# Sums of w_down's quarters: from accumulating DMAs spread over the attention stages to GpSimd additions beside the first span's w_up products

## The chip, the cores and the metric

The kernel runs on one core of a Trainium2 chip. The metric is the device time of one execution in microseconds (us). The kernel before was timed in three runs: 2850.33, 2852.82 and 2859.31 us, so its median is 2852.82 us. The engines are named as the profile names them: PE (matrix products), PEld (PE's weight load), DVE (VectorE), ACT (ScalarE), POOL (GpSimd) and SP (the queue that starts nearly all DMAs).

## The reference, cut to what matters

One layer over 2048 prompt rows and 32 sample rows: projections, dilated attention and a gated MLP branch, then the feed-forward part, which is what the change concerns:

```python
h2 = rms_norm(x, norm_pre_ffn)
f = jnp.square(jax.nn.relu(h2 @ w_up)) @ w_down      # w_up 1024x4096, w_down 4096x1024, float32
x = x + rms_norm(f, norm_post_ffn)
```

## The kernel before

**Spans and stages.** The rows are worked in two spans: span 0 is 1024 prompt rows and the 32 sample rows, span 1 the other 1024. First come attention and gated branches of span 0, then those of span 1; then `ffn()` runs `up(0)` (w_up products of span 0), `down(0)`, `up(1)` and `down_rows(1)`. Every float32 product is made of three products of float32r parts (high and low).

**Seven products for eight.** In `ffn()` each matrix is cut in four quarters, and a product of two such matrices is made of seven products of quarters or of sums of quarters (`SEVEN`, line 50). On the weight side four sums are needed, named in `SUMS`: s1 = a21 + a22, s2 = a11 + s1, s3 = a11 + a21, s4 = a12 + s2. The sums depend on the weights alone. They are made ahead and laid in DRAM: `gate_sums` (of a part of w_in), `up_sums` and `down_sums` (four forms of 2048x512 each).

**How the sums are made before.** `weight_sums()` (line 1425) lists 4 blocks of w_in, 8 of w_up and 8 of w_down. For each block and each of its four sums it issues two DMAs: a plain copy DRAM to DRAM on SP's queue (line 1454), and an addition done by the DMA itself, issued by POOL with `accum_op=add` (line 1459). The generator stands in lane 3; `pace` (line 310) takes one step of it each time 3600 columns have gone through PE. So these DMAs are spread over the attention and gate stages; those of w_down come last, beside span 1's attention, its gated branch and its seven-product gates (`mix_seven`). `ffn()` empties lane 3 before its first product.

**Lanes.** A lane is a queue of generators. `tick()` takes a step of lanes 0, 1 and 2; `up` calls it twice in each of its 112 products (16 column groups by 7 forms). What a step of lane 2 issues is kept behind what stands already on PE, DVE, ACT and POOL (`ORDERED`); SP is not among them, and there the program's scheduler sets the order.

**The stream of weights in `up(0)`.** `weight_stream` (line 1512) loads two forms (128x512 each) into one of two `raw` tiles by two DMAs on SP's queue (line 283). For each form ACT casts the high part into a `wf` tile (line 1509) and POOL subtracts to get the low part (line 1510). There are four `wf` tiles. A product then takes 24 matrix instructions (line 1599) into one of three PSUM tiles `pd`, which DVE or ACT add into `ov` (lines 1606 and 1608). After the sixth and the seventh form of a column group the results go to DRAM in `f` (lines 1636 and 1639). At the same time lane 1 carries `moved()` and `differences(1)`, which make span 1's input `h2` and its differences `hd` (lines 385, 1377, 1467 to 1472).

**Small tiles that the change uses.** The pool `sm` has two tiles of 128x1024 floats with the tags `t` and `gbc` and one buffer each. They hold scratch rows and gain rows in other stages; during `up(0)` the kernel before uses neither, but for the load of the last gain into `gbc` (line 451).

Of the kernel before, what the change touches and what calls it, by code (L numbers as in the profile page):

```python
# [10 lines left out]
F32 = mybir.dt.float32  # L11
F32R = mybir.dt.float32r
AF = mybir.ActivationFunctionType
ALU = mybir.AluOpType
# [4 lines left out]
P = 128  # L19
D = 1024  # L20
# [38 lines left out]
    ("s4", "b22", ((X12, X12),)),  # L59
)  # L60
SUMS = ("s1", "s2", "s3", "s4")
DIFFS = ("t1", "v", "t3", "t4")


# [48 lines left out]
def hybrid_step(ctx: ExitStack, tc: tile.TileContext, ins: dict, outs: list):  # L113
    nc = tc.nc
# [92 lines left out]
    def push(lane, gen):  # L207
        lanes[lane].append(gen)
        return gen
# [28 lines left out]
    def drain(lane, gen=None):  # L238

        while (lanes[lane] if gen is None else gen in lanes[lane]) and step(lane):  # L240
            pass
# [1186 lines left out]
    def weight_sums():  # L1428
# [5 lines left out]
        def by_rows(name, dst):  # L1434
            w = ins[name][0]
            hk, hm = w.shape[0] // 2, w.shape[1] // 2
            n = hk // 8
            for q in range(8):
                u, l = slice(q * n, (q + 1) * n), slice(hk + q * n, hk + (q + 1) * n)
                todo.append(parts(w[u, :hm], w[l, :hm], w[u, hm:], w[l, hm:], [dst[i, u] for i in range(4)]))  # L1440
# [5 lines left out]
            u, l = slice(q * P, (q + 1) * P), slice(512 + q * P, 512 + (q + 1) * P)  # L1446
            todo.append(parts(w[u, ca], w[l, ca], w[u, cb], w[l, cb], [gate_d[i, u] for i in range(4)]))
        by_rows("w_up", up_d)
        by_rows("w_down", down_d)
        for n in range(len(todo) + 2):  # L1450
            for i in range(4):
                if n < len(todo):
                    with tc.issue_after(load[0].ins):
                        nc.sync.dma_start(todo[n][i][0], todo[n][i][1])
                    yield

                j = n - (2 if i == 3 else 1)
                if 0 <= j < len(todo):
                    nc.gpsimd.dma_start(todo[j][i][0], todo[j][i][2], accum_op=ALU.add, max_dma_last_dim=8192)
                    yield  # L1460

    def differences(s):

# [35 lines left out]
    def down_form(form, k, nk, m, nm):  # L1499

        if form in SUMS:
            src = down_d[SUMS.index(form), k * P : (k + nk) * P, m : m + nm]
        else:
            i, j = int(form[1]) - 1, int(form[2]) - 1
            src = ins["w_down"][0][j * 2048 + k * P : j * 2048 + (k + nk) * P, i * 512 + m : i * 512 + m + nm]
        return src.rearrange("(k p) m -> p k m", p=P)
# [17 lines left out]
    def ffn():  # L1524
# [293 lines left out]
        ops.update(prepare(0, ("s2",), forms[6:]))  # L1818
        for gen in later:
            push(1, gen)  # L1820
        up(0, ops)
        drain(0)
        drain(1)
        ops1 = {}
        gain_last = {}

# [123 lines left out]
```

## Time and profile before

| | |
|---|---|
| median of 3 runs | 2852.82 us |
| the profiled execution | 2853.56 us |
| its span from first to last instruction | 2851.9 us, so 1.7 us lie around it |
| PE busy | 2805.7 us, 98% of the span |
| POOL busy | 1329.6 us, 47% |
| DVE / ACT busy | 1375.0 us / 1288.6 us |
| DMA | 550.95 MB, mean 193 GB/s |
| `up(0)` | from about 1546 to 1873 us of the span |

A row of the windows view gives a stretch of the span, its length, the busy time of PE, PEld, DVE, ACT and POOL (with the number of instructions), the granted PE clock as a share, the mean busy share of the core's 16 DMA engines and the GB/s that they moved. A row of the waits view names who waited, for whom, and us in total, times, and the longest. A row of the groups view gives line, engine, operation, tiles and shapes, the count, then busy us and mean ns of one. The chain of waits is followed back from the last instruction.

### The profile page before, as it was taken

Reading aid. Unit: us, or ns where it says so; the run is one execution under the profiler, and the core shown is the slowest. Engines: PE = TensorE matmul, PEld = TensorE weight load, DVE = VectorE, ACT = ScalarE, POOL = GpSimd, SP = SyncE. Lnnn points to the kernel's source line nnn. Section 1 sums busy time; section 2 is a strip of 40 time slices with the busy share of each in tenths; the row PEclk is TensorE's granted clock in tenths of the full one; section 3 lists DMA queues with packets and bytes.
Section 4 is the critical chain, followed back from the end, with each engine's and each line's share of the span. In section 5 each row is a group of like instructions: output and inputs, shape, how many; then the busy total and the mean of one; then the engine's idle time right before and its main releaser. Section 6 shows DMA issues by size and latency. Waiting matters only on the chain.

```text
span 2851.9 us, 45811 instructions
## 1 busy us (share of the span) xinstructions
PE 2805.7 (98%) x17350; PEld 2551.3 (89%) x17350; DVE 1375.0 (48%) x2318; ACT 1288.6 (45%) x2519; POOL 1329.6 (47%) x1167
## 2 busy tenths in 40 slices
PE   8999999999999999999999999999999999999998
PEld 8999999999988888877888999999999888888887
DVE  4557464752544434554555546442424644452225
ACT  5444452213654444433346544453434544554334
POOL 3346434564123444444761444455546644445553
PEclk9999999999999999999999999999999999999999
DMA  4344345875677665499867878676656766586665
GB/s 140 104 126 136 93 126 162 221 203 152 206 196 217 167 157 150 121 221 271 227 177 253 278 233 297 197 257 194 214 177 218 235 202 193 185 283 195 190 188 169
DMA packets 486606, 550.95 MB, mean 193 GB/s; under 512 B 28273, under 2 KB 373425, under 8 KB 476658
## 3 DMA queue, kind: packets, MB, share of 16 engines
q1 hardware_dynamic: 472992, 502.60, 55.0%
q0 software_dynamic: 13248, 45.36, 8.7%
q8 instruction: 137, 2.24, 0.3%
q14 instruction: 83, 0.68, 0.1%
q10 hardware_dynamic: 146, 0.07, 0.0%
HBM read 425.54 MB, written 206.27 MB: 222 GB/s over the span
## 4 chain that ended last, share of the span: by engine, by line
PE 84%; DVE 6%; DMA 5%; ACT 2%; issue 2%; POOL 1%; SPq 0%; DVEq 0%; POOLq 0%; ACTq 0%
PE pg L323 25%; PE pd L1599 22%; PE pe L1599 11%; PE pe L1707 10%; PE pg L337 5%; PE pg L1236 2%; PE pu L757 2%; PE pt L743 1%; DMA gbc<-in_cache_kv_w_dram 1%; PE ps L323 1%; PE ps L709 1%; DMA raw<-in_w_in_dram 1%; PE ps L710 1%; POOL wf L1510 1%; PE pt L366 1%
## 5 line engine op out<-in xcount | busy, mean ns | idle before, releaser
L1510 POOL TENSOR_TENSOR wf<-raw,wf 128x512 fp32r<-128x512 f32 x493 | 699.8, 1426 | 725.8 <-ACT wf L1509 688.3
L323 PE MATMUL pg<-act,wh 128*128 128x352 f32 (+2 forms) x2976 | 796.4, 346 | 2.4 <-DVE xt L1292 1.4
L323 PEld LDWEIGHTS pg<-act,wh 128*128 128x128 f32 x2976 | 522.3, 189 | 32.5 <-DVE xt L1292 1.7
L1509 ACT CAST wf<-raw 128x512 fp32r<-128x512 f32 x493 | 304.7, 619 | 531.0 <-PE pd L1599 182.8
L323 PE MATMUL pg<-act,wl 128*128 128x352 f32 (+3 forms) x1488 | 512.5, 345 | 0.0
L303 POOL TENSOR_TENSOR wl<-raw,wh 128x512 fp32r<-128x512 f32 (+1 forms) x184 | 242.2, 1345 | 300.9 <-ACT wh L299 262.5
L1599 PE MATMUL pd<-act,wf 128*128 128x264 f32 x2880 | 361.2, 285 | 1.3 <-ACT ov L196 1.0
L1599 PEld LDWEIGHTS pd<-act,wf 128*128 128x128 f32 x2880 | 354.0, 189 | 2.0 <-ACT ov L196 1.4
L323 PEld LDWEIGHTS pg<-act,wl 128*128 128x128 f32 x1488 | 280.2, 188 | 17.1
L1707 PE MATMUL pe<-wf,act 128*128 128x512 f32 (+1 forms) x984 | 224.3, 389 | 1.4 <-ACT wf L1509 1.2
L1707 PEld LDWEIGHTS pe<-wf,act 128*128 128x128 f32 x984 | 181.7, 188 | 43.1 <-ACT wf L1509 1.4
L1608 DVE TENSOR_TENSOR ov<-pd,ov 128x528 f32<-128x528 f32 x140 | 96.2, 704 | 193.4 <-PE pd L1599 188.2
L1599 PE MATMUL pd<-pair,wf 128*128 128x264 f32 x1440 | 183.2, 284 | 0.0
L1599 PE MATMUL pe<-act,wf 128*128 128x512 f32 x768 | 182.6, 392 | 0.1
L1510 DVE TENSOR_TENSOR act<-flat,act 128x1024 fp32r<-128x1024 f32 (+1 forms) x76 | 102.1, 1346 | 162.4 <-ACT act L1509 162.4
L1599 PEld LDWEIGHTS pd<-pair,wf 128*128 128x128 f32 x1440 | 177.9, 188 | 0.0
L1599 PEld LDWEIGHTS pe<-act,wf 128*128 128x128 f32 x768 | 143.8, 188 | 32.9 <-ACT pair L1509 0.3
L299 ACT CAST wh<-raw 128x1024 fp32r<-128x1024 f32 (+1 forms) x91 | 91.7, 1009 | 173.3 <-PE pg L323 94.3
L1608 DVE TENSOR_TENSOR ov<-pe,ov 128x512 f32<-128x512 f32 x136 | 91.5, 687 | 137.3 <-PE pe L1599 126.4
L1599 PE MATMUL pd<-oa,wf 128*128 128x264 f32 x1056 | 135.0, 284 | 0.0
L715 ACT ACTIVATE ov<-ov 128x256 f32<-128x256 f32 (+1 forms) x192 | 91.8, 478 | 92.9 <-DVE ov L711 90.4
L1599 PEld LDWEIGHTS pd<-oa,wf 128*128 128x128 f32 x1056 | 130.8, 188 | 0.0
(340 smaller groups left out, 4619.4 us busy)
## 6 DMA issues: line engine op xcount, KB each, us to landing
raw<-in_w_in_dram SPq DMA_DIRECT2D x70, 512.0 KB
raw<-up_sums SPq DMA_DIRECT2D x128, 256.0 KB
raw<-down_sums SPq DMA_DIRECT2D x128, 256.0 KB
flat<-f SPq DMA_DIRECT2D x48, 528.0 KB
raw<-in_w_up_dram SPq DMA_DIRECT2D x96, 256.0 KB
raw<-in_w_down_dram SPq DMA_DIRECT2D x96, 256.0 KB
flat<-f SPq DMA_DIRECT2D x48, 512.0 KB
f<-ov SPq DMA_DIRECT2D x16, 1056.0 KB
```

The lines of the kernel that those rows point to most:

```text
L299: nc.scalar.copy(wh[:, :o], raw[:, :o])
L303: eng.tensor_tensor(wl[:, c], raw[:, c], wh[:, c].bitcast(F32), ALU.subtract)
L323: nc.tensor.matmul(pt[:, :n], a[:, o : o + P], b, start=(i == 0 and j == 0), stop=(i == last and j == 2))
L337: nc.tensor.matmul(pt[:n, o : o + width], a, b, start=(i == 0 and j == 0), stop=(i == last and j == 2))
L715: nc.scalar.activation(pb[:, h, :w], pb[:, h, :w], AF.Exp, scale=-1.0, bias=stats[:, u, h : h + 1], accum_out=stats[:, u, 2 + h : 3 + h],)
L757: nc.tensor.matmul(up[:, hs], tb[:, h, e * P : (e + 1) * P], vv[:, hs], start=(e == 0), stop=(e == len(rows) - 1),)
L1236: nc.tensor.matmul(pt, w[:, c, k], x[k][:, d], start=k == 0 and j == 0, stop=k == 3 and j == 2)
L1509: nc.scalar.copy(high, raw)
L1510: eng.tensor_tensor(low, raw, high.bitcast(F32), ALU.subtract)
L1599: nc.tensor.matmul(pt[:, o : o + n], w[:, a], x[:, b, c : c + n], start=first and j == 0, stop=last and j == 2)
L1608: nc.vector.tensor_tensor(X[to], res, X[add], ALU.add)
L1707: nc.tensor.matmul(pts[i][:, cs], x[k][:, c, t * P : (t + 1) * P], w[:, d, 0, cs], start=k == 0 and j == 0, stop=k == 15 and j == 2,)
```

## The change

`by_rows("w_down", ...)` is taken out of `weight_sums`, so lane 3 has 12 blocks left for 20. A new generator `down_sums` is pushed on lane 2 ahead of `up(0)`, and lane 2 is emptied behind it. It works in 32 blocks, each of 128 rows by 256 columns of every quarter. A block is loaded by two DMAs (2 x 256 KB) into the tile `t` or `gbc` in turn, POOL makes the four sums in place with four additions of 128x256, and one DMA of 512 KB stores all four to `down_sums`. The load of block n+2 into the same tile comes four steps behind the first additions of block n; a block takes six steps. The four forms lie in another order in DRAM (`DOWN_SUMS`). The rest of the sums (w_in, w_up) stay as they are.

```diff
+DOWN_SUMS = ("s2", "s4", "s3", "s1")
...
         by_rows("w_up", up_d)
-        by_rows("w_down", down_d)
...
+    def down_sums():
+
+        def fetch(n):
+            x = sm.tile([P, D], F32, tag=("t", "gbc")[n % 2], bufs=1, name="sums")
+            x = x.rearrange("p (i j m) -> p i j m", i=2, j=2)
+            k, c = n // 2, slice(n % 2 * 256, n % 2 * 256 + 256)
+            for j in range(2):
+                src = ins["w_down"][0][j * 2048 + k * P : j * 2048 + (k + 1) * P]
+                nc.sync.dma_start(x[:, :, j, :], src.rearrange("p (i m) -> p i m", i=2)[:, :, c])
+            return x, down_d[:, k * P : (k + 1) * P, c].rearrange("s p m -> p s m")
+
+        loaded = [fetch(0), fetch(1)]
+        for _ in range(6):
+            yield
+        for n in range(32):
+            x, dst = loaded[n]
+            a11, a12, a21, a22 = x[:, 0, 0], x[:, 0, 1], x[:, 1, 0], x[:, 1, 1]
+            nc.gpsimd.tensor_tensor(a22, a21, a22, ALU.add)
+            nc.gpsimd.tensor_tensor(a21, a11, a21, ALU.add)
+            yield
+            nc.gpsimd.tensor_tensor(a11, a11, a22, ALU.add)
+            nc.gpsimd.tensor_tensor(a12, a12, a11, ALU.add)
+            nc.sync.dma_start(dst, x.rearrange("p i j m -> p (i j) m"))
+            for _ in range(3):
+                yield
+            if n < 30:
+                loaded.append(fetch(n + 2))
+            yield
+            yield
...
-            src = down_d[SUMS.index(form), k * P : (k + nk) * P, m : m + nm]
+            src = down_d[DOWN_SUMS.index(form), k * P : (k + nk) * P, m : m + nm]
...
+        push(2, down_sums())
         up(0, ops)
-        drain(0)
-        drain(1)
+        for lane in range(3):
+            drain(lane)
```

In the changed kernel the new lines are 1470 (loads), 1479, 1480, 1482 and 1483 (additions) and 1484 (store); lines behind them are 30 higher than before (L1510 becomes L1540, L1599 L1629, L1636 and L1639 L1666 and L1669), lines between the two edits 1 higher (L283 becomes L284).

**POOL, as `up(0)` begins and in its last third.** Before, POOL ends the loads of w_out's parts (`wl`, `oa`, `pair`) and then has nothing but the low parts of the weight stream, 214 in a row, through `up(0)` and into `down(0)`:

```order
L1255 TENSOR_TENSOR ov<-ov,xt 128x512
L303 TENSOR_TENSOR oa<-raw,oa 128x512 x2
L303 TENSOR_TENSOR pair_13784<-raw,pair_13784 128x512 x2
L303 TENSOR_TENSOR pair_13785<-raw,pair_13785 128x512 x2
L303 TENSOR_TENSOR pair_13786<-raw,pair_13786 128x512 x2
L303 TENSOR_TENSOR wl<-raw,wh 128x512 x2
L1510 TENSOR_TENSOR wf<-raw,wf 128x512 x214
```

Now the four additions of a block stand between every three or four of them:

```order
L1540 TENSOR_TENSOR wf<-raw,wf 128x512 x4
L1479 TENSOR_TENSOR sums<-sums 128x256
L1480 TENSOR_TENSOR sums<-sums 128x256
L1482 TENSOR_TENSOR sums<-sums 128x256
L1540 TENSOR_TENSOR wf<-raw,wf 128x512
L1483 TENSOR_TENSOR sums<-sums 128x256
L1540 TENSOR_TENSOR wf<-raw,wf 128x512 x3
L1479 TENSOR_TENSOR sums<-sums 128x256
L1480 TENSOR_TENSOR sums<-sums 128x256
L1482 TENSOR_TENSOR sums<-sums 128x256
L1483 TENSOR_TENSOR sums<-sums 128x256
L1540 TENSOR_TENSOR wf<-raw,wf 128x512 x4
```

Counted over POOL's whole order, the first block's fourth addition stands behind the 4th low part of `up(0)`, the last block's behind the 109th of 112.

**SP, in the last third of `up(0)`.** Before, its queue holds the loads of the weight stream (`raw`) and the stores of the results (`f_116`):

```order
L1639 DMA f_116<-ov 128x2112
L283 DMA raw<-up_sums 128x4x128 x3
L283 DMA raw<-in_w_up_dram 128x4x128 x2
L1636 DMA f_116<-ov 128x1584
L283 DMA raw<-up_sums 128x4x128
L1639 DMA f_116<-ov 128x2112
L283 DMA raw<-in_w_up_dram 128x4x128
L283 DMA raw<-up_sums 128x4x128 x3
```

Now each block's store and the next load into the same tile stand among them, with two to four other DMAs between the store and that load:

```order
L1484 DMA down_sums<-sums 128x4x256
L1470 DMA sums<-in_w_down_dram 128x2x256 x2
L284 DMA raw<-up_sums 128x4x128 x2
L1484 DMA down_sums<-sums 128x4x256
L284 DMA raw<-up_sums 128x4x128
L284 DMA raw<-in_w_up_dram 128x4x128
L1470 DMA sums<-in_w_down_dram 128x2x256 x2
L1666 DMA f_116<-ov 128x1584
L284 DMA raw<-in_w_up_dram 128x4x128
L284 DMA raw<-up_sums 128x4x128
L1484 DMA down_sums<-sums 128x4x256
L1669 DMA f_116<-ov 128x2112
```

The load must wait for the store of the same tile to land, and what stands behind it on SP's queue waits too.

**SP, late in span 1's gated branch.** Before, the copies for the sums stand among the loads of w_ao and w_bo and the scratch stores `gt` and `pb`:

```order
L283 DMA raw<-in_w_ao_dram 128x2x128
L283 DMA raw<-in_w_bo_dram 128x4x128
L1137 DMA gt<-gbc 128x512
L1454 DMA down_sums<-in_w_down_dram 256x512
L1189 DMA pb<-xt 128x1024
L1150 DMA gt<-gt 128x512
L1189 DMA pb<-xt 128x1024
L283 DMA raw<-in_w_ao_dram 128x2x128
L283 DMA raw<-in_w_bo_dram 128x4x128
L1137 DMA gt<-junk 128x512
L1454 DMA down_sums<-in_w_down_dram 256x512
```

Now they are gone, and the rest has closed up in a slightly different order (here and in PE's own order the scheduler exchanges neighbouring pieces; the instructions are the same):

```order
L284 DMA raw<-in_w_ao_dram 128x2x128
L284 DMA raw<-in_w_bo_dram 128x4x128
L1138 DMA gt<-gbc 128x512 x2
L1151 DMA gt<-gt 128x512
L1190 DMA pb<-xt 128x1024
L284 DMA raw<-in_w_ao_dram 128x2x128
L284 DMA raw<-in_w_bo_dram 128x4x128
L1138 DMA gt<-junk 128x512
L1190 DMA pb<-xt 128x1024
L1138 DMA gt<-gbc 128x512 x2
L284 DMA raw<-in_w_in_dram 128x4x128 x2
```

## The prediction

> **What bounds the kernel now.** I read the page first, then the windows view by stage, then PE's own waits in the stages that the change touches. The page's first line:
>
> ```profile
> PE 2805.7 (98%) x17350; PEld 2551.3 (89%) x17350; DVE 1375.0 (48%) x2318; ACT 1288.6 (45%) x2519; POOL 1329.6 (47%) x1167
> ```
>
> PE is idle for only 2851.9 - 2805.7 = 46 us of the span. No gain can come but from these gaps, and a change that makes PE wait loses at once. The windows view shows where w_down's sums lie today (1034 to 1440 us; the last two stages of that time are quoted) and where they go (`up(0)`):
>
> ```profile
> 1170.00:1310.00 140.00, 134.58 (x607) 108.97 (x606) 84.08 (x147) 54.89 (x76) 67.58 (x68) 0.98 0.80 207
> 1310.00:1460.00 150.00, 140.66 (x604) 113.47 (x603) 91.17 (x108) 65.62 (x111) 94.92 (x77) 0.99 0.87 231
> 1546.00:1873.00 327.00, 325.65 (x2673) 324.35 (x2672) 173.52 (x219) 164.18 (x275) 147.86 (x109) 1.00 0.77 251
> ```
>
> In the old place PE idles 140 - 134.58 = 5.4 us and 150 - 140.66 = 9.3 us; the DMA engines are at 0.80 and 0.87. In the new place PE idles 1.35 us in 327, with the DMA engines at 0.77 and 251 GB/s, and POOL is free for more than half of the time. PE's waits in the two old stages, in order of the rows above:
>
> ```profile
> PE pg L323 <- POOL wl L303: 1.7, 1, 1.7
> PE ps L323 <- DVE xt L1179: 1.6, 1, 1.6
> ...
> PE pg L1236 <- DVE xt L1243: 7.2, 3, 2.8
> PE pg L1236 <- DVE gx L1243: 2.2, 1, 2.2
> ```
>
> The reader is to see that most of it (9.4 us) is PE waiting for DVE, which empties its banks in `mix_seven`; no DMA is named.
>
> **What is taken away.** 32 copies on SP's queue, 32 accumulating DMAs on POOL's:
>
> ```profile
> L1454 SPq DMA_DIRECT2D down_sums<-in_w_down_dram x32: 496/582/1975, 1034.2 to 1400.6; - x32
> L1459 POOL DMA_DIRECT2D down_sums<-in_w_down_dram x16 | 14.9, 929 | 0.0
> L1459 POOL DMA_DIRECT2D down_sums<-down_sums x16 | 12.8, 798 | 6.9 <-DMA gt<-junk 5.9 <-DMA down_sums<-in_w_down_dram 1.0
> ```
>
> That is 14.9 + 12.8 = 27.7 us of POOL, 32 x 0.58 = 19 us of SP, and 64 DMAs of 512 KB, over some 400 us in which neither engine is the bound. On PE's path I count only the stall between 1240 and 1280 us, where the DMA share is over 1 and PE waits for a low part of w_ao/w_bo:
>
> ```profile
> 1240.00:1260.00 20.00, 17.09 (x71) 12.71 (x69) 13.96 (x21) 4.67 (x7) 8.55 (x12) 0.94 0.83 192
> 1260.00:1280.00 20.00, 18.93 (x73) 15.00 (x74) 15.12 (x18) 4.45 (x9) 7.75 (x8) 0.89 1.07 298
> ```
>
> It holds 2.91 + 1.07 = 4.0 us idle, and the lower clock around it costs 0.06 x 17.09 + 0.11 x 18.93 = 3.1 us: 7.1 us. Half of it is DVE's own work (the `xt` wait), so I take -4 us. The bounds: at best all 7.1 us and the 2.2 us of `gx`, -9; at worst nothing goes and the exchanged order there costs as much again as half of it, +4. The other waits for DVE stay.
>
> **What is put into `up(0)`: POOL's own time.** The trace has no addition of 128x256 in POOL. The nearest rows are an addition of 128x128 and, in the stretch of `up(0)`, the low parts of 128x512:
>
> ```profile
> L831 POOL TENSOR_TENSOR o<-o,junk 128x128 f32<-128x128 f32 x32 | 16.5, 517 | 2.2
> L1510 POOL TENSOR_TENSOR wf<-raw,wf 128x512 fp32r<-128x512 f32 x109 | 147.9, 1359 | 234.9 <-ACT wf L1509 225.7 <-DMA raw<-in_w_up_dram 5.1 <-DMA raw<-up_sums 4.2
> ```
>
> On the straight line between 0.52 and 1.36 us, 256 columns cost 0.52 + (1.36 - 0.52)/3 = 0.80 us; the ends 0.52 and 1.36 are the bounds. 128 additions x 0.80 = 102 us, so POOL works 148 + 102 = 250 of 327 us, 76% (66% to 98% at the bounds). As throughput this is hidden beside PE: 0 us. One product takes 2.91 us, from two low parts one after the other (start, us; below them ACT's casts ahead of the low parts):
>
> ```profile
> 1713.46 1.29 POOL L1510 TENSOR_TENSOR wf<-raw,wf 128x512 fp32r<-128x512 f32 x1 [1.61 <-ACT wf L1509]
> 1716.37 1.29 POOL L1510 TENSOR_TENSOR wf<-raw,wf 128x512 fp32r<-128x512 f32 x1 [1.61 <-ACT wf L1509]
> ...
> L1509 ACT CAST wf<-raw 128x512 fp32r<-128x512 f32 x110 | 67.9, 619 | 123.9 <-PE pd L1599 75.3 <-POOL wf L1510 19.3 <-DMA raw<-in_w_up_dram 17.4
> ```
>
> With four `wf` tiles a low part is due three products (8.7 us) behind the release of its tile and takes 0.62 + 1.36 = 2.0 us with ACT's cast. So a low part may come some 6.7 us late before PE stands still. Four additions in a row (3.2 us) fit in that; a load that POOL must wait for may not.
>
> **Bytes.** 64 loads of 128x2x256 and 32 stores of 128x4x256 floats are 33.6 MB. `up(0)` moves 251 GB/s x 327 us = 82.1 MB today, so 115.7 MB, 354 GB/s for the same 327 us. What the engines have done with PE fully busy:
>
> ```profile
> 1720.00:1740.00 20.00, 20.00 (x167) 20.00 (x166) 12.62 (x16) 9.95 (x17) 9.16 (x8) 1.00 0.97 332
> 1885.00:1900.00 15.00, 15.00 (x125) 15.00 (x124) 7.54 (x8) 6.66 (x11) 5.48 (x4) 1.00 1.01 373
> ```
>
> At 373 GB/s it takes 310 us and costs nothing; at 332 it takes 348 us, +21 us. So the stage goes from 0.77 to about full.
>
> **The turn of a tile.** This is the term that I expect to decide. A tile is loaded, added, stored, and loaded again, and each step waits for the one before. POOL's order holds 31 blocks in 105 products, 105 x 2.91 / 31 = 9.9 us a block and 19.7 us for a turn of one of the two tiles. How long a DMA takes to land is seen where the chain of waits runs through one; first two beside the old sums, then two at the quiet end of the kernel (start, us):
>
> ```profile
> 1405.19 6.32 DMA raw<-in_w_in_dram
> 1421.93 7.74 DMA raw<-in_w_in_dram
> ...
> 2801.56 3.80 DMA raw<-down_sums
> 2810.84 3.78 DMA raw<-down_sums
> ```
>
> And issuing on SP, the median of the stretch, and three issues in a row where the DMA engines are full:
>
> ```profile
> L283 SPq DMA_DIRECT2D raw<-up_sums x60: 359/482/1464, 1552.9 to 1864.3; - x60
> 1709.27 3.52 SPq L283 DMA_DIRECT2D raw<-up_sums  x3
> ```
>
> A turn is two landings, four additions (3.2 us), one low part between them (1.36 us), and three issues that nothing covers (the store's, the load's, one DMA ahead), 3 x 0.48 = 1.4 to 3.5 us. With a full stage I take the landings of the crowded rows, 6.32 + 7.74 = 14.1 us. The sum is 14.1 + 3.2 + 1.36 + 1.4 = 20.1 us at the light price of an issue and 22.2 us at the heavy one. Over 31/2 = 15.5 turns that is 0.4 x 15.5 = 6 us and 2.5 x 15.5 = 39 us more than the 19.7 us at hand. `up(0)` has full and light quarters (0.97 above, 0.77 in the mean), so I take the middle, +22 us. With the quiet landings the turn is 12.2 us and costs nothing. It is the same lateness as that of the bytes, counted once.
>
> Who waits: the reload (L1470) waits on SP for the store of its tile, and behind it on SP stand the weight loads (L284) and the results' stores (L1666, L1669). The first addition (L1479) waits on POOL for the load, and behind it stand the low parts that PE needs. How little room the weight loads have today (waits, 1600 to 1866 us):
>
> ```profile
> POOL wf L1510 <- ACT wf L1509: 137.3, 83, 5.7
> ...
> ACT wf L1509 <- DMA raw<-in_w_up_dram: 17.4, 5, 6.6
> ...
> PE pd L1599 <- DVE ov L1608: 0.3, 1, 0.3
> ```
>
> ACT has already waited 6.6 us for a weight load, about the whole slack of 6.7 us, without PE noticing. There is no second 6 us.
>
> **Behind `up(0)`.** `down(0)` reads the sums first here, 45 us behind the stage's end, so the last store has time: 0 us.
>
> ```profile
> 1918.02 0.88 SPq L283 DMA_DIRECT2D raw<-down_sums  x2
> ```
>
> **Sum.** -4 + 22 = +18 us on the profiled execution's 2853.56 us (0.7 us above the median): about 2871 us on the median's scale. About 0.3% (8.6 us) is what a measurement of this kernel can tell from no change.
>
> **The rivals.** (1) The stage takes it in: landings stay at 6 us or less, or the scheduler's spacing leaves SP something else to wait for anyway. For it: PE stayed fully busy in the rows at 0.97 and 1.01. Then only the -4 us are left: 2849 us. The Trainium skill, DMA: Bandwidth & Descriptors, section Specifications, puts HBM's limit for one core at about 358 GB/s; by that the 354 GB/s would just fit and the bytes would cost nothing. The trace has a 15 us stretch above it (373 GB/s), so the page and the trace leave this rival open, and speak for no more than a bare fit. (2) Faster: the stage takes it in, and the old place frees more than I count: the whole -9 us and 1 or 2 us of the 7.2 us `xt` waits, if those banks are emptied late because loads come late. 2843 us. It decides from the point at which `mix_seven`'s DVE work, not its loads, stops being last; the waits quoted name DVE, which speaks against it. (3) A convoy: POOL waits for loads in order, the low parts behind it come late, and the heavy price of an issue holds throughout with a second low part in each turn: 22.2 + 1.36 = 23.6 us, 3.9 x 15.5 = 60 us; between the 39 us and this, +50, it gives 2899 us.
>
> **How the numbers follow.** Forecast 0.45, (1) 0.28, (2) 0.10, (3) 0.17. The forecast is slower by over 0.3% for 0.43 of its 0.45 and the same for 0.02; (1) is the same for 0.25 and faster for 0.03; (2) is faster; (3) is slower. Faster 0.13, same 0.27, slower 0.60. The range runs from (1)'s and part of (2)'s times, 2845, up to 2906, which is 2853 - 4 + 57, near the upper end of (3).
>
> **What would show it.** In the changed profile: a row for `up(0)` with PE idle of 15 us and more, PE waiting for `wf` (L1540), POOL idle ahead of L1479 with a DMA as releaser, SP waiting at L1470 for `down_sums<-sums`, and a DMA share near 1. The stall between 1240 and 1280 us should be smaller. I am wrong if PE's idle time in `up(0)` stays under 5 us, or if SP's waits at L1470 are long and PE does not care; and wrong about the old place if PE's idle time there does not move or falls by more than 9 us.

## The result, and the profile after

The changed kernel is slower by 0.7%: median 2873.94 us of 4 runs (2871.73 to 2877.58) against 2854.52 us of the kernel before (4 runs, 2850.33 to 2859.31), ratio 1.0068 (95% interval 1.0056 to 1.008). That is +19.4 us where +18 was forecast. The profiled execution took 2874.18 us with a span of 2872.5. The sum came out; two of its terms did not.

The page's first line, after. PE is idle for 2872.5 - 2813.7 = 58.8 us of the span, 46 before; POOL has 92.6 us more work in 128 - 32 = 96 more instructions:

```profile
PE 2813.7 (98%) x17350; PEld 2557.5 (89%) x17350; DVE 1384.5 (48%) x2318; ACT 1285.7 (45%) x2519; POOL 1422.2 (50%) x1263
```

The windows of the old place (two stages) and the new one, after; columns as in the rows of before:

```profile
1170.00:1310.00 140.00, 137.75 (x632) 112.24 (x630) 82.58 (x143) 57.83 (x82) 57.73 (x54) 1.00 0.33 107
1310.00:1460.00 150.00, 149.74 (x725) 125.07 (x724) 92.47 (x114) 71.00 (x114) 93.99 (x69) 1.00 0.51 157
1546.00:1873.00 327.00, 307.82 (x2463) 303.58 (x2462) 169.33 (x199) 139.62 (x236) 237.49 (x219) 0.98 0.96 321
```

In the old place the DMA share fell from 0.80 and 0.87 to 0.33 and 0.51, and PE's idle time with it: from 5.4 and 9.3 us to 2.3 and 0.3. In the new place the share rose from 0.77 to 0.96, and PE's idle time from 1.35 to 19.2 us.

Fixed windows mix stages once a kernel runs ahead or late. So I measure by milestones of PE's own order: the first product of `up(0)` (the group that writes `pd`) and the first product of `up(1)` (`pe`). Before and after, each with count, min/median/max ns, then first and last start in us:

```profile
L1599 PE MATMUL pd<-act,wf x2880: 279/284/389, 1550.1 to 2209.5; 128*128 128x264 f32 x192
L1599 PE MATMUL pe<-act,wf x768: 387/391/477, 2216.5 to 2524.5; 128*128 128x512 f32 x192
```

```profile
L1629 PE MATMUL pd<-act,wf x2880: 278/284/559, 1532.6 to 2229.1; 128*128 128x264 f32 x192
L1629 PE MATMUL pe<-act,wf x768: 387/391/477, 2236.1 to 2544.2; 128*128 128x512 f32 x192
```

`up(0)` starts 1550.1 - 1532.6 = 17.5 us earlier: this is what the old place gave back. From there to `up(1)` it takes 703.5 us for 666.4: 37.1 us more. Behind `up(1)`'s start nothing moved (635.4 us to the end of the span before, 636.4 after). The windows between those two milestones (their ends lie some 1.2 us short of the second), before and after:

```profile
1550.10:2215.30 665.20, 664.85 (x5480) 664.30 (x5480) 302.86 (x343) 312.72 (x491) 332.40 (x230) 1.00 0.71 233
```

```profile
1532.60:2235.00 702.40, 676.28 (x5480) 670.33 (x5481) 319.22 (x343) 308.11 (x490) 447.97 (x358) 0.99 0.81 267
```

For the same 5480 matrix instructions PE idles 26.1 us instead of 0.35, and is busy 676.3 instead of 664.9 us. So the pauses are in part paid a second time. A long one, with the 40 us behind it:

```profile
1720.00:1760.00 40.00, 33.94 (x263) 32.29 (x262) 23.78 (x28) 16.40 (x29) 28.73 (x25) 0.99 1.04 351
1760.00:1800.00 40.00, 39.94 (x318) 39.73 (x317) 26.54 (x28) 15.84 (x27) 31.32 (x28) 0.96 1.02 350
```

In the second row PE is hardly idle, but does 318 instructions where 40 us at a clock of 1.00 hold 333: the clock granted there is 0.96. Not every pause is followed by that, and the mean clock of 0.99 accounts for only some 7 of the 11.4 us (an estimate: 0.01 x 676); the rest is not traced.

Who waits there, from 1530 to 1910 us after (us in total, times, longest), by engine in the order PE, ACT, POOL, SP, DVE:

```profile
PE pd L1629 <- DVE ov L1638: 8.7, 3, 4.8
PE pd L1629 <- ACT wf L1539: 7.0, 6, 2.7
PE pd L1629 <- POOL wf L1540: 5.0, 7, 1.1
...
ACT wf L1539 <- DMA raw<-in_w_up_dram: 49.3, 15, 6.6
ACT wf L1539 <- DMA raw<-up_sums: 46.5, 23, 5.3
...
POOL sums L1479 <- DMA sums<-in_w_down_dram: 28.3, 14, 5.5
...
SPq L1470 <- DMA down_sums<-sums: 27.2, 11, 5.6
...
DVE ov L1638 <- DMA f<-ov: 7.4, 1, 7.4
```

The longest of these waits lead back to transfers. ACT waits 95.8 us for weight loads, 38 times (26.8 us and 9 times before, from 1548 to 1910 us); POOL 28.3 us for blocks, with low parts queued behind; SP 27.2 us for a tile's store, with weight loads queued behind. DVE waits 7.4 us once for a result store `f`, until 1595.4 us, and PE's longest pause (4.8 us, until 1596.3) hangs on that.

A pause of another kind, near 1740 us: the block's load in the chain of waits, POOL's timeline, PE's timeline (start, us, and in brackets the idle time ahead and its releaser):

```profile
1731.80 7.89 DMA sums<-in_w_down_dram
```

```profile
1739.82 0.74 POOL L1479 TENSOR_TENSOR sums<-sums 128x256 f32<-128x256 f32 x1 [5.52 <-DMA sums<-in_w_down_dram]
...
1742.47 1.75 POOL L1540 TENSOR_TENSOR wf<-raw,wf 128x512 fp32r<-128x512 f32 x1
```

```profile
1741.64 0.76 PE L1629 MATMUL pd<-act,wf 128*128 128x264 f32 x4 [0.96 <-ACT wf L1539]
...
1744.27 2.70 PE L1629 MATMUL pd<-act,wf 128*128 128x264 f32 x20 [0.83 <-POOL wf L1540]
```

The load takes 7.89 us to land, POOL stands 5.52 us for it, makes three additions, and only then the low part that PE needs; PE pauses 0.83 us. This is the convoy of the forecast's rival (3), seen whole; one such pause is short.

### The profile page after: what moved, and what is told of

Same layout as the page of the kernel before. It is cut to its first block, busy times and chain, and to the rows that moved or that the text cites. A ratio compares the mean times of both kernels' runs of the same rounds, so it can differ in the third digit from the quotient of the medians.

```text
span 2872.5 us, 46044 instructions
## 1 busy us (share of the span) xinstructions
PE 2813.7 (98%) x17350; PEld 2557.5 (89%) x17350; DVE 1384.5 (48%) x2318; ACT 1285.7 (45%) x2519; POOL 1422.2 (50%) x1263
## 5 line engine op out<-in xcount | busy, mean ns | idle before, releaser
L1540 POOL TENSOR_TENSOR wf<-raw,wf 128x512 fp32r<-128x512 f32 x493 | 705.3, 1436 | 612.3 <-ACT wf L1539 563.3
L1629 PE MATMUL pd<-act,wf 128*128 128x264 f32 x2880 | 368.7, 287 | 16.3 <-ACT wf L1539 6.4
L1629 PEld LDWEIGHTS pd<-act,wf 128*128 128x128 f32 x2880 | 359.0, 191 | 19.5 <-ACT wf L1539 7.6
L1629 PE MATMUL pd<-pair,wf 128*128 128x264 f32 x1440 | 185.8, 285 | 3.3 <-ACT junk L397 1.5
L1629 PEld LDWEIGHTS pd<-pair,wf 128*128 128x128 f32 x1440 | 178.8, 188 | 4.6 <-issue 1.7
L1629 PE MATMUL pe<-act,wf 128*128 128x512 f32 x768 | 182.6, 392 | 0.1
L1540 DVE TENSOR_TENSOR act<-flat,act 128x1024 fp32r<-128x1024 f32 (+1 forms) x76 | 102.6, 1353 | 162.3 <-ACT act L1539 157.8
L1629 PEld LDWEIGHTS pe<-act,wf 128*128 128x128 f32 x768 | 143.8, 188 | 32.9 <-issue 0.3
L1629 PE MATMUL pd<-oa,wf 128*128 128x264 f32 x1056 | 136.8, 285 | 6.2 <-DVE ov L1638 4.0
L1629 PEld LDWEIGHTS pd<-oa,wf 128*128 128x128 f32 x1056 | 131.3, 189 | 7.5 <-DVE ov L1638 3.6
```

The lines of the kernel that those rows point to most:

```text
L1540: eng.tensor_tensor(low, raw, high.bitcast(F32), ALU.subtract)
L1629: nc.tensor.matmul(pt[:, o : o + n], w[:, a], x[:, b, c : c + n], start=first and j == 0, stop=last and j == 2)
```

## The experiments

The theories, by their letters in the expectations. On the new place: the turn of a tile decides (A, the forecast's own); the bytes decide (B); POOL's additions slow what runs beside them (C); or the number of DMAs on SP's queue decides (F). On the old place: the whole DMA load made the loss, copies and accumulations alike (D), or POOL's accumulating DMAs alone, by the time that POOL spends issuing them (E) or by the addition in them. Each run is set against the kernel before on the same chip; "start" is the start of `up(0)`, "length" the time from there to the start of `up(1)`, both of one profiled execution. Runs 8 and 10 have the same old place and start 4.6 us apart, so a few us between two starts are scatter.

| run | median us | before | ratio (95%) | start | length |
|---|---|---|---|---|---|
| before | | | 1 | 1550.1 | 666.4 |
| the change | 2873.94 | 2854.52 | 1.0068 (1.0056 to 1.008) | 1532.6 | 703.5 |
| 1 no sums of w_down | 2839.10 | 2852.64 | 0.9951 (0.9936 to 0.9966) | 1533.2 | 667.4 |
| 2 copies only | 2837.29 | 2852.64 | 0.9948 (0.9933 to 0.9962) | 1529.7 | 666.8 |
| 3 no additions | 2858.83 | 2852.64 | 1.0022 (1.0009 to 1.0034) | 1551.0 | 678.7 |
| 4 additions only | 2841.27 | 2852.64 | 0.9954 (0.9938 to 0.9971) | 1534.5 | 668.8 |
| 5 third tile | 2862.94 | 2852.43 | 1.0039 (1.0024 to 1.0054) | 1534.0 | 690.8 |
| 6 half the bytes | 2849.18 | 2852.43 | 0.9991 (0.998 to 1.0001) | 1530.1 | 677.3 |
| 7 old sums earlier | 2858.22 | 2852.43 | 1.002 (1.0008 to 1.0031) | 1558.1 | 666.8 |
| 8 half in each place | 2850.09 | 2852.43 | 0.9999 (0.999 to 1.0009) | 1542.1 | 674.3 |
| 9 plain copies on POOL | 2845.98 | 2854.62 | 0.9969 (0.9959 to 0.9979) | 1541.1 | 666.9 |
| 10 half, third tile | 2848.49 | 2854.62 | 0.9981 (0.9971 to 0.9991) | 1537.5 | 673.5 |
| 11 third tile, half the bytes | 2852.68 | 2854.62 | 0.9992 (0.9981 to 1.0004) | 1536.0 | 683.0 |
| 12 half, third tile, held back | 2845.37 | 2855.15 | 0.9967 (0.9955 to 0.9979) | 1537.5 | 670.6 |

**1. No sums of w_down.** From the kernel before; the four sum forms are read from the plain matrix instead, so `down_sums` is neither made nor read:

```diff
-        by_rows("w_down", down_d)
...
-            src = down_d[SUMS.index(form), k * P : (k + nk) * P, m : m + nm]
+            i = SUMS.index(form)
+            src = ins["w_down"][0][i // 2 * 2048 + k * P : i // 2 * 2048 + (k + nk) * P, i % 2 * 512 + m : i % 2 * 512 + m + nm]
```

> The kernel before without w_down's sums at all (left out; the products that use them read plain quarters of w_down in their place). In the changed kernel up(0) starts at 1532.6 us for 1550.1 before (-17.5), and up(0) with down(0) takes 703.5 us for 666.3 (+37.2). If the -17.5 us come from taking the old sums away, up(0) starts here at about 1533 us, up(0) with down(0) stays at 666 us, and the time is about 2837 us. Rival: the gain comes from the scheduler's exchanged order in the changed program and not from the sums; then up(0) starts at 1545 to 1550 us and the time is 2850 us or more.

`up(0)` starts at 1533.2, 16.9 us earlier than before, and the median falls 13.5 us. The old sums therefore cost some 14 to 17 us, not 4; the change gets the same start (1532.6) by taking them away. Its loss in `up(0)` is then 2873.94 - 2839.10, about 35 us.

**2. Copies only.** SP's 32 copies stay, POOL's 32 accumulating DMAs go; sum forms from the plain matrix as in run 1:

```diff
-                if 0 <= j < len(todo):
+                if 0 <= j < min(len(todo), 12):
```

> The kernel before with w_down's 32 copies on SP's queue, but without the 32 accumulating DMAs on POOL's (so the sums are left out; the products read plain quarters). Theory D, the DMA engines' load in the old place makes PE wait: half of the load is left, so up(0) starts half way, at about 1541 us, 2846 us in all. Theory E, POOL held by issuing the accumulating DMAs (27.7 us) makes the low parts late: all of it is gone, up(0) starts at 1533 us, 2837 us in all.

The old place's first stage in run 1 and in run 2:

```profile
1170.00:1310.00 140.00, 137.75 (x634) 112.35 (x633) 83.15 (x147) 57.27 (x80) 57.70 (x54) 1.00 0.33 107
```

```profile
1170.00:1310.00 140.00, 137.76 (x631) 112.19 (x630) 80.40 (x142) 59.04 (x85) 56.34 (x53) 1.00 0.60 183
```

The copies bring 76 GB/s more and PE is busy to the same 0.01 us. The medians lie within each other's spread. So copies on SP's queue alone cost nothing measurable, and the whole loss of the old place goes when POOL's accumulating DMAs go, as theory E had it (run 9 asks what in them it is). Theory D falls as it was put (half of the load, half of the loss). That a load costs only where copies and POOL's DMAs come together is not excluded: the share is 0.60 here and 0.80 before.

**3. No additions.** The changed kernel with its loads and stores, and without the four additions (what is stored are the quarters themselves):

```diff
-            nc.gpsimd.tensor_tensor(a22, a21, a22, ALU.add)
-            nc.gpsimd.tensor_tensor(a21, a11, a21, ALU.add)
...
-            nc.gpsimd.tensor_tensor(a11, a11, a22, ALU.add)
-            nc.gpsimd.tensor_tensor(a12, a12, a11, ALU.add)
```

> The changed kernel without POOL's 128 additions; loads and stores of the 32 blocks stay (the quarters are stored unsummed). Theory A, the turn of a tile (load, add, store, reload): the turn loses 3 us of additions and the wait for a low part between them, 22 to 18 us, under the 19.7 us at hand: up(0) with down(0) falls from 703 to 666 to 675 us, 2838 to 2847 us in all. Theory B, the bytes fill the DMA engines: nothing changes, 700 us, 2871 us. Theory C, POOL's time and the port that it shares with DVE: 666 us, 2837 us.

Transfers without additions cost 2858.83 - 2839.10 = 19.7 us over run 1. But the start moved too (1551.0): with no additions to hold them, the stores and reloads slid ahead of `up(0)`, as windows of run 3 show:

```profile
1460.00:1480.00 20.00, 16.48 (x108) 13.81 (x107) 1.12 (x2) 5.16 (x6) 11.20 (x9) 1.00 0.78 241
...
1540.00:1560.00 20.00, 14.21 (x78) 12.93 (x77) 11.51 (x14) 13.20 (x33) 3.88 (x3) 0.83 0.99 346
```

In the same stretches run 1 idles 0 us. The run shows that transfers alone make a loss, not how much of the change's 37 us is theirs: the order of the transfers is another one, the length (678.7) fits none of the three forecasts, and the profiled execution was the slowest of its eight.

**4. Additions only.** The changed kernel with the first two loads and all 128 additions, and no other load or store; sum forms from the plain matrix:

```diff
-            nc.sync.dma_start(dst, x.rearrange("p i j m -> p (i j) m"))
...
-            if n < 30:
-                loaded.append(fetch(n + 2))
+            loaded.append(loaded[n])
```

> The changed kernel with the 128 additions, but loads of the first two blocks alone and no stores (so no sums reach memory; the products read plain quarters). Theories A and B: no transfer to wait for, up(0) with down(0) at 666 to 668 us, 2837 to 2839 us in all. Theory C (POOL's time, DVE kept waiting at the shared port): most of the 37 us stays, 690 us and more, over 2860 us.

The stage's window, then POOL's first addition and DVE's second operation of `differences`, in run 4; last the same DVE operation before:

```profile
1534.50:1861.50 327.00, 324.45 (x2673) 323.85 (x2674) 187.17 (x217) 163.37 (x273) 262.44 (x238) 1.00 0.76 250
```

```profile
L1479 POOL TENSOR_TENSOR sums<-sums 128x256 f32<-128x256 f32 x32 | 27.8, 870 | 0.0
...
L1506 DVE TENSOR_TENSOR ov<-ov 128x528 f32<-128x528 f32 x15 | 15.9, 1061 | 0.5
```

```profile
L1478 DVE TENSOR_TENSOR ov<-ov 128x528 f32<-128x528 f32 x15 | 12.1, 804 | 0.5
```

DVE is slowed beside POOL's additions (804 to 1061 ns), but PE is busy 324.45 of 327 us and the whole costs 2841.27 - 2839.10 = 2.2 us, within the runs' spread. Theory C falls as the cause. The Trainium skill, SBUF — State Buffer, section Who interferes with whom, says that a DVE instruction with two SBUF inputs contends with a GpSimd instruction that reads SBUF; these rows agree.

**5. A third tile.** The changed kernel with every third block in an unused part of `ov`, and loads three blocks ahead:

```diff
+            if n % 3 == 2:
+                x = ov[:, 14 * (TMAX // 2) : 14 * (TMAX // 2) + D]
+            else:
+                x = sm.tile([P, D], F32, tag=("t", "gbc")[n % 3], bufs=1, name="sums")
...
-            if n < 30:
-                loaded.append(fetch(n + 2))
+            if n < 29:
+                loaded.append(fetch(n + 3))
```

> The changed kernel with a third tile for the blocks (a free piece of ov), so that a tile has three blocks' time for its turn, 29.6 us for 19.7; bytes, DMAs and additions stay. Theory A, the turn of a tile decides: up(0) with down(0) falls from 703 to 666 to 675 us, 2838 to 2847 us in all. Theory B, the bytes decide: it stays at 695 us or more, 2865 us or more.

SP's wait for the store of a tile, then the stage's window, in run 5:

```profile
SPq L1473 <- DMA down_sums<-sums: 4.3, 4, 1.5
```

```profile
1534.00:1861.00 327.00, 310.57 (x2492) 306.66 (x2493) 178.31 (x204) 149.11 (x254) 250.26 (x229) 0.98 1.01 333
```

SP's wait for stores is all but gone (4.3 us for 27.2 at the reload; 0.9 us more for the third tile, and once 5.3 us at the load of the last gain into `gbc`), and 37.1 us became 690.8 - 666.4 = 24.4, between the two forecasts and nearer that of the bytes. The rest stays with no turn to blame: the DMA engines are at 1.01 and move 333 GB/s over the whole stage. A good part of it is one pause of 7.1 us near 1599 us, where DVE waits 8.6 us for a store of `f`.

**6. Half the bytes.** The changed kernel with blocks of 128 columns for 256 (half the sums are made), in as many DMAs and additions; sum forms from the plain matrix:

```diff
-            k, c = n // 2, slice(n % 2 * 256, n % 2 * 256 + 256)
+            k, c = n // 2, slice(n % 2 * 256, n % 2 * 256 + 128)
...
-                nc.sync.dma_start(x[:, :, j, :], src.rearrange("p (i m) -> p i m", i=2)[:, :, c])
+                nc.sync.dma_start(x[:, :, j, :128], src.rearrange("p (i m) -> p i m", i=2)[:, :, c])
```

> The changed kernel with half of each block's columns loaded, added and stored (half of the sums are left out; the products read plain quarters). The count and order of the DMAs and additions stay, the bytes fall to 82.1 + 16.8 = 98.9 MB, 302 GB/s. Theory B, bytes: up(0) with down(0) at 666 to 672 us, 2837 to 2843 us in all. Theory A, turn: landings and additions are shorter by some 3 to 5 us of 22, so at most half of the 37 us is left, 670 to 685 us, 2841 to 2856 us. Theory F, the number of DMAs on SP's queue: 695 us or more, 2865 us or more.

SP's wait for stores, then the stage and its worst stretch, in run 6:

```profile
SPq L1470 <- DMA down_sums<-sums: 37.6, 18, 3.4
```

```profile
1530.10:1857.10 327.00, 317.02 (x2603) 315.54 (x2604) 162.59 (x209) 158.67 (x267) 210.18 (x235) 1.00 0.91 293
...
1560.00:1600.00 40.00, 34.74 (x286) 34.16 (x285) 19.45 (x26) 19.04 (x32) 23.85 (x29) 1.00 1.02 332
```

The loss in length falls from 37.1 to 10.9 us although SP waits longer for stores than in the change (37.6 us for 27.2). But 677.3 us lies in the range that the turn theory gave (670 to 685), not in that of the bytes (666 to 672): half the bytes can also shorten a landing, and with it the turn (POOL's wait for blocks fell from 28.3 to 11.3 us). Run 6 alone can't part the two; run 5, where 24.4 us stay without the turn, says that it is not the larger part. About half of what is left lies in 40 us, where the share is still 1.02. (The additions are also halved in width; by run 4 all of them cost about 2 us.)

**7. The old sums earlier.** The kernel before, lane 3 stepped every 2700 columns:

```diff
-SUM_EVERY = 3600
+SUM_EVERY = 2700
```

> The kernel before with a step of the old sums each 2700 columns for 3600, so that they end at about 1170 us for 1438 us, ahead of the seven-product gates. If the old sums cost time only where they run beside the end of the gated branch and the seven-product gates, up(0) starts at about 1535 us and the time is about 2840 us. Rival: the denser DMAs make PE wait as much in the stages ahead of it, and the time stays at 2852 us.

The copies for w_down in run 7 (count, min/median/max ns, first and last start):

```profile
L1454 SPq DMA_DIRECT2D down_sums<-in_w_down_dram x32: 497/605/8677, 882.1 to 1283.8; - x32
```

The last copy now starts at 1283.8 us and the last accumulating DMA at 1329.6, as the gates begin. The gates (`mix_seven`) take 137.4 us for 147.0; but they start 17.4 us later (1329.5 for 1312.1), and the median is 5.8 us worse than before, worse than either forecast. Moving the accumulating DMAs to earlier stages moves their cost along; it isn't only the old slot that is at fault.

**8. Half in each place.** The changed kernel; half of w_down's blocks go back to the accumulating DMAs, the other 16 on-chip blocks take twelve steps each:

```diff
+        w = ins["w_down"][0]
+        for q in range(4):
+            u, l = slice(q * 256, q * 256 + 256), slice(2048 + q * 256, 2304 + q * 256)
+            dst = [down_d[DOWN_SUMS.index(s), u] for s in SUMS]
+            todo.append(parts(w[u, :512], w[l, :512], w[u, 512:], w[l, 512:], dst))
...
-        for n in range(32):
+        for n in range(16, 32):
```

> Half and half: the sums of w_down's first 1024 rows of each quarter by the old DMAs (they end at about 1236 us), the other half by the new blocks on the chip, 16 blocks at twelve steps each for 32 at six. Theories A and B alike: a tile has 35 us for its turn and the stage moves 302 GB/s, so up(0) with down(0) takes 666 to 670 us, and up(0) starts at 1533 to 1540 us: 2837 to 2848 us in all, ahead of both kernels. If half of the transfers cost half of the 37 us all the same, it is 2855 us.

Start 1542.1, halfway between 1550.1 and 1532.6; length +7.9 us, more than the 0 to 4 us that both theories gave, and far less than half of 37.1. The gates are as short as in the change; what is left of the old cost lies ahead of them (they start at 1315.4 us for 1305.9). In the new place the loss falls faster than the load; a tile also has twice the time for its turn here, so the run doesn't say which of the two does it. The sum is that of the kernel before (0.9999).

**9. Plain copies on POOL.** The kernel before, w_down's 32 DMAs on POOL without the addition (`down_sums` gets plain quarters), sum forms from the plain matrix:

```diff
-                    nc.gpsimd.dma_start(todo[j][i][0], todo[j][i][2], accum_op=ALU.add, max_dma_last_dim=8192)
+                    nc.gpsimd.dma_start(
+                        todo[j][i][0], todo[j][i][2], max_dma_last_dim=8192,
+                        **({"accum_op": ALU.add} if j < 12 else {}),
+                    )
```

> The kernel before with w_down's 32 accumulating DMAs turned into plain copies of the same shapes, still issued by POOL (so the sums are left out; the products read plain quarters). Without these 32 DMAs the time was 2837 us, with them accumulating 2852 us. If POOL's issuing of them or their place in its queue costs the 15 us, nothing changes: up(0) starts at about 1550 us, 2852 us in all. If it is the addition itself in the DMA engines (16.8 MB take some 96 us of all 16 engines' time, 175 GB/s, for 320 GB/s of plain transfers), up(0) starts at 1533 to 1538 us, 2837 to 2842 us in all.

POOL's queue from 1170 to 1460 us (packets, MB, share of the 16 engines) and the time from issue to landing of one half of its DMAs, before and in run 9:

```profile
q0 software_dynamic: 5168, 16.25, 32.5%
...
down_sums<-down_sums POOLq DMA_DIRECT2D x16, 512.0 KB, 6.6
```

```profile
q0 software_dynamic: 3376, 16.25, 17.2%
...
down_sums<-down_sums POOLq DMA_DIRECT2D x16, 512.0 KB, 4.7
```

The same 16.25 MB hold the engines for 0.172 x 290 = 50 us instead of 0.325 x 290 = 94. `up(0)` starts at 1541.1, between the two forecasts: of the 16.9 us between the kernel before and run 1, 9.0 go with the addition and 7.9 stay with plain copies on POOL. (By the medians 8.6 of 13.5 us go. With the scatter of the starts, it is about half.) POOL also spends less time on issuing them, 9.2 + 8.3 = 17.5 us for 27.7, so the half that goes is not the addition in the DMA engines alone for certain. Run 2 showed SP's plain copies to cost nothing. What in POOL's copies costs the 7.9 us (their issue on POOL, or that they come on top of SP's) no run separates.

**10. Half in each place, with a third tile.** Run 8 and the third tile of run 5.

```diff
-        loaded = {16: fetch(16), 17: fetch(17)}
+        loaded = {n: fetch(n) for n in (16, 17, 18)}
```

> Half and half again (first 1024 rows of each quarter summed by the old DMAs, 16 blocks on the chip at twelve steps each), with the third tile. Half and half alone took 2850.1 us, with up(0) starting at 1542 us and up(0) with down(0) at 674 us, 8 us over the kernel before. If those 8 us are the turn of a tile, they go: 667 us, 2843 us in all, ahead of both kernels. If they are the bytes, nothing changes: 2850 us.

0.9981 (0.9971 to 0.9991), length +7.1 us: at half the load the third tile does little for the length. The old place is that of run 8, so the earlier start (1537.5 for 1542.1) is none of its doing.

**11. Third tile and half the bytes.** Runs 5 and 6 together.

```diff
+            if n % 3 == 2:
+                x = ov[:, 14 * (TMAX // 2) : 14 * (TMAX // 2) + D]
...
+                nc.sync.dma_start(x[:, :, j, :128], src.rearrange("p (i m) -> p i m", i=2)[:, :, c])
```

> The changed kernel with both the third tile and half of each block's columns (half of the sums are left out; the products read plain quarters). The third tile alone left 24 us of the 37 in up(0) and down(0), half the bytes alone 11. If turn and bytes are all there is, both together leave 0 to 4 us: up(0) with down(0) at 666 to 670 us, 2837 to 2841 us in all. If the number of DMAs on SP's queue costs something by itself, 675 us or more stays, 2846 us or more.

The expectation of 0 to 4 us fell, and the sign of its rival came: 16.6 us of length stay, more than in run 6 (10.9). By the medians runs 6 and 11 can't be told apart. But the run did not take the turn away. SP's waits for stores ahead of a reload, from 1530 to 1910 us:

```profile
SPq L1473 <- DMA down_sums<-sums: 25.6, 11, 4.6
...
SPq L1473 <- DMA down_sums<-ov: 10.7, 5, 2.9
```

That is 36.3 us, as in run 6 (37.6) and not as in run 5. So bytes, turn and number of DMAs stay unparted here. For the number (F) speaks a comparison at the same bytes: runs 6 and 11, with 96 DMAs, lose 10.9 and 16.6 us of length; runs 8 and 10, with 48 of twice the size, lose 7.9 and 7.1. (There a block also has twelve steps for six, so it may be the time for a turn as well.) Where the loss of run 11 lies, in 40 us rows:

```profile
1560.00:1600.00 40.00, 33.38 (x269) 32.89 (x268) 19.42 (x30) 18.09 (x29) 26.66 (x35) 0.96 1.03 336
...
1640.00:1680.00 40.00, 39.65 (x328) 39.44 (x327) 16.67 (x21) 16.57 (x29) 22.90 (x28) 1.00 0.80 249
```

The same blocks cost 0.35 us of idle time where the share is 0.80, and 6.6 us at 1560 to 1600. Before, that stretch (there 10 to 50 us into `up(0)`, in run 11 24 to 64) already moved 305 GB/s with PE fully busy:

```profile
1560.00:1600.00 40.00, 40.00 (x331) 39.79 (x331) 24.60 (x33) 24.08 (x45) 19.21 (x14) 1.00 0.93 305
```

So the loss is uneven, and the largest piece meets the start of `up(0)`, where the kernel's own loads of `h` and stores of `f` stand. The share alone doesn't decide, as the next run shows.

**12. Held back from the crowd.** Run 10, its first block some 40 steps later and a block every eleven steps for twelve:

```diff
-        for _ in range(6):
+        for _ in range(46):
             yield
```

> Half and half with the third tile, and the 16 blocks on the chip held back by 40 steps more (about 58 us), so that they begin when up(0)'s own crowded start is over (the kernel before moves 305 GB/s there); a block takes eleven steps for twelve. Without the delay up(0) with down(0) took 673.5 us, 7 us over the kernel before, and PE lost 5.5 us between 1530 and 1600 us. If what is lost is the meeting of the blocks with crowded stretches, the loss in the first 70 us of up(0) goes: up(0) with down(0) at 667 to 669 us, 2842 to 2845 us in all. If it is the bytes of the whole stage, nothing changes: 673 us, 2848 us.

The first 80 us of `up(0)` and one later stretch, in run 10 and in run 12 (both start at 1537.5):

```profile
1537.50:1577.50 40.00, 37.49 (x295) 37.31 (x296) 27.48 (x29) 27.27 (x50) 30.83 (x21) 0.96 0.96 314
1577.50:1617.50 40.00, 38.04 (x304) 37.86 (x302) 22.81 (x28) 17.49 (x28) 21.32 (x20) 0.96 0.99 345
...
1697.50:1737.50 40.00, 40.00 (x333) 40.00 (x332) 25.52 (x30) 18.95 (x31) 24.93 (x22) 1.00 1.04 351
1737.50:1777.50 40.00, 40.00 (x332) 40.00 (x331) 23.20 (x30) 18.58 (x31) 24.59 (x23) 1.00 1.05 362
```

```profile
1537.50:1577.50 40.00, 37.97 (x300) 37.76 (x301) 23.67 (x29) 26.38 (x50) 19.00 (x13) 0.96 0.94 302
1577.50:1617.50 40.00, 40.00 (x334) 40.00 (x333) 24.99 (x30) 18.12 (x29) 20.86 (x17) 1.00 0.87 292
```

PE's idle time in the first 80 us falls from 4.5 to 2.0 us, and the pause behind a store of `f` near 1599 us, 2.0 us in run 10 and 3 to 7 us in the change and in runs 5, 8 and 11, is gone. In run 10 all the idle time up to 1897 us lies in these 80 us; 80 later us at 351 and 362 GB/s, more than the start moves, cost nothing. So a full share isn't enough to make PE wait; it costs where an engine needs one of the transfers at once, as DVE does there with the store of `f`. Length +4.2 us, for +7.1 in run 10: between the forecast (667 to 669 us, it was 670.6) and its rival (673). The median, 2845.37 us at 0.9967 (0.9955 to 0.9979), is faster than the kernel before and 1% below the change (0.9967 / 1.0068). It makes all sums. That it is faster than run 10 (0.9971 to 0.9991) isn't clear of the noise. The other runs that come as low (1, 2, 4 and 9) make no sums, or not all of them.

## Why the prediction was right, and where it was wrong

**PE bounds the kernel, and only its gaps count: right.** The profiled executions differ by 20.6 us, and -17.5 + 37.1 + 1.0 (old place, new place, behind) makes that up; in both places it is PE's gaps that moved, with the lower clock beside them.

**The old place, -4 us: wrong, it was -17.5.** Two steps failed. The first is "On PE's path I count only the stall between 1240 and 1280 us". The gates behind it took 147.0 us before (1312.1 to 1459.1) and 135.6 after (1305.9 to 1441.5): 11.4 of the 17.5 us lay there. The second is that a wait that names DVE was taken for DVE's own work, twice. In the stall, "Half of it is DVE's own work (the `xt` wait)" took 7.1 us down to 4; nearly all of it went (after, PE idles 0.8 us there at a clock of 1.00), and the gates begin 6.2 us earlier. (Of the stall's two rows only the second has a DMA share over 1; the larger idle time, 2.91 us, stands at 0.83.) In the gates, "most of it (9.4 us) is PE waiting for DVE ... no DMA is named" led to "The other waits for DVE stay". They did not: after, the same stage has

```profile
PE pg L1237 <- DVE xt L1244: 0.3, 1, 0.3
```

A releaser is the last link of a chain. One engine further up, in the gates of the kernel before (1312 to 1459 us) and of the changed one, ACT's waits were:

```profile
ACT wf L1509 <- DMA raw<-in_w_in_dram: 26.6, 8, 6.4
```

```profile
ACT wf L1539 <- PE pg L1237: 40.3, 22, 2.2
```

Before, the weight stream waits for its loads; after, for PE to free a tile, as it should. And DVE's own additions in those gates took longer beside the accumulating DMAs, before and after:

```profile
L1254 DVE TENSOR_TENSOR xt<-xt,pbx 128x512 f32<-128x512 f32 x6 | 9.8, 1627 | 12.8 <-ACT xt L1246 8.2 <-DMA pbx<-pb 4.6
```

```profile
L1255 DVE TENSOR_TENSOR xt<-xt,pbx 128x512 f32<-128x512 f32 x7 | 6.9, 987 | 3.0 <-ACT xt L1247 3.0
```

Rival (2) had this mechanism ("if those banks are emptied late because loads come late"), priced it at 1 or 2 us, and held the row that named DVE against it. The rows of ACT were there to be read. Run 1 confirms the size without the new work, run 2 shows that it goes with POOL's DMAs while SP's copies stay, and run 9 splits it about in half between the addition and POOL's transfers as such. In run 9 the same additions on DVE take 1084 ns for 1627 (x6 each) and ACT waits 7.5 us for `w_in`, so the slow DVE and most of the wait for loads go with the addition in the DMAs (or with POOL's longer issue of them); in which way it slows DVE no run tells.

**POOL's additions, 0.80 us each and hidden: right.** They took 0.87 us in the mean in run 4 and 0.89 in the change, at best 0.72, and cost about 2 us, within the runs' spread.

**Bytes and turn, +22 us, "the same lateness as that of the bytes, counted once": the direction was right, the size 15 us short (37.1).** The turn came out near: the first additions of 32 blocks start over 1881.2 - 1534.1 = 347.1 us, 22.4 us for a turn of two tiles, where 20.1 to 22.2 were forecast. That is the pace of the whole stage as well, though, and only 11 of the 30 reloads waited on SP for a store. (With the quiet landings the sum is 13.5 us and not 12.2, which left the issues out; it changes nothing.) What failed is the counting once, and the middle. The third tile takes SP's wait away and 12.7 us with it; 24.4 stay, above the +21 that the bytes alone were given at 332 GB/s. Halving the bytes takes 26.2 and leaves a longer wait for stores. So the turn is a loss of its own and the smaller one. The larger goes with the traffic put in; bytes and number of DMAs are not parted (run 11), and it lies in a few pauses more than in the mean of the stage (run 12). Of the two rows that bounded the bytes, the 15 us stretch at 373 GB/s misled: over 327 us run 5 moved 333 at a share of 1.01, so the 332 row was nearer to what the stage sustained. The Trainium skill, DMA: Bandwidth & Descriptors, section Specifications, gives a limit of about 358 GB/s for one core, which I weighed for rival (1). Short stretches passed it (362 GB/s over 40 us in run 10), no whole stage here reached it, and the "bare fit" was none.

**"There is no second 6 us": right in substance, and not only for weight loads.** ACT's longest wait for a load stayed at 6.6 us, but it waited 38 times for 9, and PE paused 6 times for ACT (7.0 us). The longest pause came by way of a result store: PE waits for a bank that DVE empties, and DVE for the store of `f` that still reads its target in `ov`. I had named these stores as queued behind the reload on SP, not who waits for them.

**Behind `up(0)`, 0 us: right** (1.0 us from `up(1)`'s start to the end).

**The sum** was near (+18 for +19.4) because -13.5 us at the old place and +15 at the new one cancelled. That is luck: neither error was seen. The signs listed under what would show it all came in `up(0)`, and the stall between 1240 and 1280 us shrank; the sign set against the reading of the old place ("falls by more than 9 us") came true as well, and it told rightly that the reading there was wrong.

## What to carry to other kernels

When PE's waits name an engine, read one link further, what that engine and the one behind it waited for, before calling a wait that engine's own work. When traffic is moved into a stage, take what the stage can move from the longest full stretch of the trace, not the best short one. Then look for the places where some engine waits for a transfer already, here the first 80 us of `up(0)`: added blocks cost there, while 80 later us at a full share cost nothing. An accumulating DMA costs more than its bytes say. Splitting such work between two places, with a third tile and away from the crowded start, beat either place alone (run 12); the plain split did not (run 8).

## What the runs showed of the hardware

- 16.25 MB of POOL's DMAs held the 16 engines for 94 us with the addition in the DMA and 50 us as plain copies (run 9); landing took 6.6 and 4.7 us for one half of them, 8.0 and 5.7 us for the other.
- 32 plain copies on SP, 76 GB/s more in a stage of PE work, cost no measurable time (run 2).
- Over 327 us run 5 moved 333 GB/s at a DMA share of 1.01. Two stretches of 40 us in a row at 351 and 362 GB/s (shares 1.04 and 1.05) left PE fully busy (run 10).
- PE's pauses were in part paid twice: in the change 25.8 us of idle time more came with 11.4 us more busy time for the same 5480 instructions, and 40 us behind a long pause ran at a granted clock of 0.96.
